# Stick-breaking scores copied to SBUF by ScalarE, the running sum subtracted from the copy; softplus and its sum share a place

## The chip, the core and the metric

The kernel runs on one core of a Trainium2 chip. The metric is the device time of one execution in microseconds, the median of several runs. The core's engines run at the same time, each through its own list of instructions in order: TensorE (PE, with its weight loads as PEld), VectorE (DVE), ScalarE (ACT), GpSimd (POOL), and SyncE (SP), which issues most DMAs. An instruction waits on semaphores for what it needs from another engine. Matmuls write to PSUM, where this kernel keeps eight tiles of 128 x 512 floats (called banks below); the rest of the working data is in SBUF.

## The reference

One decoder layer on a sequence of 512 positions with width 2048. Two attention groups of 16 heads each work on one projection of the normed input, a sliding-window group A and a stick-breaking group B. Their normed outputs go through one output projection, and a squared-ReLU MLP follows. The change is in group B, which for a block of 128 queries is:

```python
z = einsum('bqhd,bshd->bhqs', q_blk, k) * scale
log_beta = log_sigmoid(z)
log_1m = where(causal, log_sigmoid(-z), 0.0)
later = cumsum(log_1m, axis=3, reverse=True) - log_1m
w = where(causal, exp(log_beta + later), 0.0)
out = einsum('bhqs,bshd->bqhd', w, v)
```

With softplus(z) = -log_sigmoid(-z) and log_sigmoid(z) = z - softplus(z), the exponent of w is z minus the sum of softplus from the end of the row to this position, this one included. That is the form that the kernel computes: softplus as max(z, 0) + ln(1 + exp(-|z|)), its running sum from the right, and exp(z - sum).

## The kernel before, in words

Everything is in float32; the large products are made of three matmuls each, from high and low parts of both operands (`mm3`, lines 113 to 118; the parts come from a cast on ACT, L91, and a subtraction on DVE, L92, whose tiles are called `hi_...` and `lo_...`). The stages follow each other: input norm, group A's projections and attention, group B's, output projection, MLP. PE runs the large projections all the time, and the attention is threaded through them: after every second 128-row tile of a projection `pump()` starts or ends one unit of attention.

A unit of group B is one block of queries i (0 to 3) of one pair of heads c (0 to 7), the two heads being the two halves s = 0 and 1. `begin(i)` computes the scores of both halves into two PSUM banks (`scores`, L549, six matmuls in all) and calls `weights`. `end(i)`, one or more pumps later, transposes the weights on PE through two more banks (`wtr`, L583), copies them on DVE to the pair's tiles `wt` (L584), and after block 3 multiplies by v (`bv`, L600). A block is (i + 1) * 128 wide. Pairs 0 to 3 run from about 325 to 456 us, beside projections `ps_v` and `ps_qk`; pairs 4 to 7 from about 500 to 632 us. The handover from one pair to the next inside such a group has block 3 of the one and block 0 of the next in flight at once.

The weights of one half take ten steps: on ACT Abs of z, Exp and Ln (L562 to L564, into tile `a`); on DVE the softplus from z and a (L565, into tile `b`); on GpSimd a select that zeroes the part of the diagonal block that is not causal (L566); on DVE the scan from the right (L569, back into `a`) and the subtraction z - a (L571, into `b`); on GpSimd a select that fills the non-causal part with -1e30 (L572); on ACT the last Exp (L574). The scores z stay in their PSUM bank until L571 has read them. The banks of all these short-lived tiles come from one pool of four (`bank`, tag `pa`), so the next tile that gets a bank waits for the last reader of the tile before it. The SBUF tiles `a` and `b` have two buffers for each tag: `wa` and `wb` for half 0, `wc` and `wd` for half 1.

The order on each engine is not written out: the framework's scheduler makes it from the program and its dependencies, and so can put steps of the two halves and of other work between each other. It is fixed when the program is built.

Of the kernel before, what the change touches and what calls it, by code (L numbers as in the profile page):

```python
# [12 lines left out]
F32 = mybir.dt.float32  # L13
F32R = mybir.dt.float32r
AF = mybir.ActivationFunctionType
ALU = mybir.AluOpType
# [4 lines left out]
P = 128  # L21
# [37 lines left out]
def hymba_layer(ctx: ExitStack, tc: tile.TileContext, x, norm_attn_g, w_in, q_norm_g, k_norm_g,  # L59
                sinks, rel_bias, swa_out_g, sb_out_g, w_out, norm_mlp_g, w_up, w_down, sel, eye, out):  # L60
    nc = tc.nc
    x, out = x[0], out[0]
# [21 lines left out]
    wk = attn.enter_context(tc.tile_pool(name="wk", bufs=2, side="right"))  # L84
# [455 lines left out]
    def sb_pair(c, q, k, vs, keep):  # L540
# [12 lines left out]
        def weights(i, sc):  # L553
            w = (i + 1) * P
            dg = slice(i * P, (i + 1) * P)
            ws = []
            for s in range(2):
                z = sc[s][:, 0:w]
                a = wk.tile([P, 512], F32, tag=("wa", "wc")[s], name=f"a{c}_{i}{s}")[:, 0:w]
                b = wk.tile([P, 512], F32, tag=("wb", "wd")[s], name=f"b{c}_{i}{s}")[:, 0:w]  # L560

                nc.scalar.activation(out=a, in_=z, func=AF.Abs)  # L562
                nc.scalar.activation(out=a, in_=a, func=AF.Exp, scale=-1.0)
                nc.scalar.activation(out=a, in_=a, func=AF.Ln, bias=1.0)  # L564
                nc.vector.scalar_tensor_tensor(out=b, in0=z, scalar=0.0, in1=a, op0=ALU.max, op1=ALU.add)  # L565
                nc.gpsimd.affine_select(out=b[:, dg], in_=b[:, dg], pattern=[[-1, P]], compare_op=ALU.is_gt,  # L566
                                        fill=0.0, base=0, channel_multiplier=1)

                nc.vector.tensor_tensor_scan(out=a[:, ::-1], data0=ones2[:, 0:1].broadcast_to([P, w]),  # L569
                                             data1=b[:, ::-1], initial=0.0, op0=ALU.mult, op1=ALU.add)  # L570
                nc.vector.tensor_tensor(out=b, in0=z, in1=a, op=ALU.subtract)  # L571
                nc.gpsimd.affine_select(out=b[:, dg], in_=b[:, dg], pattern=[[-1, P]], compare_op=ALU.is_gt,  # L572
                                        fill=NEG, base=0, channel_multiplier=1)
                nc.scalar.activation(out=b, in_=b, func=AF.Exp)  # L574
                ws.append(b)
            return ws

        def turn(i, ws):
# [8 lines left out]
        def begin(i):  # L587
            ws_of[i] = weights(i, scores(i))
# [27 lines left out]
    for o in range(2):  # L616
        vs = v_group(o)
        for hq in range(2):
# [12 lines left out]
            for pr, (q, k) in enumerate(((q0, k0), (q1, k1))):  # L631
                c = 2 * qd + pr
# [284 lines left out]
    wd = w_down.rearrange("(g r p) n -> r p g n", r=2, p=P)  # L917
# [125 lines left out]
    for cj in range(2 * NC):  # L1043
        c, j = divmod(cj, 2)
# [7 lines left out]
        for s, (name, ai, _, b, more) in enumerate(d_products(cj)):  # L1052
# [27 lines left out]
            if not more:  # L1080
                pool, tag = ((pa, "pa"), (pp, "pp"))[b // 2]
                banks[b] = [pool.tile([P, 512], F32, tag=tag, name=f"ps_d{q}{tt}") for tt in range(2)]
            a = act[c, ai]
# [45 lines left out]
```

## Time and profile before

| | |
|---|---|
| median of 3 runs | 2007.57 us (2007.29 to 2007.81) |
| profiled execution | 2007.77 us, its span 2006.0 us |
| PE busy | 1978.6 us, 99% |
| DVE busy | 1643.7 us, 82% |
| ACT busy | 1037.7 us, 52% |
| GpSimd busy | 1020.5 us, 51% |
| TensorE's granted clock, mean | 0.998 |

Busy time of the four engines adds up to much more than the span, since they overlap. An engine's share is a mean over stages, so what a step costs is read from the stretch in which it runs. In a timeline row the first number is the start in microseconds from the start of the span, the second the length from the first start to the last end of a group of equal instructions in a row ("x2" is two of them), and the brackets name the idle time ahead of it and what ended that.

### The profile page before, as it was taken

Reading aid. Unit: us, or ns where it says so; the run is one execution under the profiler, and the core shown is the slowest. Engines: PE = TensorE matmul, PEld = TensorE weight load, DVE = VectorE, ACT = ScalarE, POOL = GpSimd, SP = SyncE. Lnnn points to the kernel's source line nnn. Section 1 sums busy time; section 2 is a strip of 40 time slices with the busy share of each in tenths; the row PEclk is TensorE's granted clock in tenths of the full one; section 3 lists DMA queues with packets and bytes.
Section 4 is the critical chain, followed back from the end, with each engine's and each line's share of the span. In section 5 each row is a group of like instructions: output and inputs, shape, how many; then the busy total and the mean of one; then the engine's idle time right before and its main releaser. Section 6 shows DMA issues by size and latency. Waiting matters only on the chain.

```text
span 2006.0 us, 31353 instructions
## 1 busy us (share of the span) xinstructions
PE 1978.6 (99%) x11652; PEld 1718.5 (86%) x11652; DVE 1643.7 (82%) x2136; ACT 1037.7 (52%) x1900; POOL 1020.5 (51%) x904
## 2 busy tenths in 40 slices
PE   8999999999999999999999999999999999999998
PEld 7877777778777889999999999998888888888887
DVE  4459754664776479999999999998999999999987
ACT  6357544553654575656565656565443333334443
POOL 0013341221321038777777777775866656656664
PEclk9999999999999999999999999999999999999999
DMA  6742332224245555665656565656766457457451
GB/s 223 114 138 85 95 103 80 81 69 136 87 140 171 196 168 179 216 203 188 204 187 208 183 212 180 215 179 251 274 250 248 159 230 283 158 223 270 147 189 63
DMA packets 213916, 350.31 MB, mean 175 GB/s; under 512 B 9779, under 2 KB 154372, under 8 KB 206596
## 3 DMA queue, kind: packets, MB, share of 16 engines
q1 hardware_dynamic: 211216, 345.02, 50.7%
q10 hardware_dynamic: 2548, 3.30, 1.4%
q8 instruction: 91, 1.49, 0.3%
q14 instruction: 61, 0.50, 0.1%
HBM read 270.16 MB, written 78.12 MB: 174 GB/s over the span
## 4 chain that ended last, share of the span: by engine, by line
PE 85%; DVE 6%; ACT 3%; DMA 3%; POOL 2%; issue 1%; SPq 0%; POOLq 0%; ACTq 0%; DVEq 0%
PE ps_u L823 10%; PE ps_u L822 10%; PE ps_u L821 10%; PE ps_d L1094 9%; PE ps_d L1095 9%; PE ps_d L1093 9%; PE ps_qk L116 3%; PE ps_qk L118 3%; PE ps_qk L117 3%; PE ps_o L118 2%; PE ps_o L116 2%; PE ps_o L117 2%; DMA skew<-rv 2%; PE bv L600 1%; DVE a L569 1%
## 5 line engine op out<-in xcount | busy, mean ns | idle before, releaser
L823 PE MATMUL ps_u<-h2h,lo_u 128*128 128x256 f32 x1792 | 507.2, 283 | 0.6 <-DVE lo_u L92 0.6
L821 PE MATMUL ps_u<-h2h,hi_u 128*128 128x256 f32 x1792 | 507.4, 283 | 0.0
L822 PE MATMUL ps_u<-h2l,hi_u 128*128 128x256 f32 x1792 | 507.1, 283 | 0.0
L1093 PE MATMUL ps_d<-hi_d,ad 128*128 128x512 f32 x896 | 349.4, 390 | 4.1 <-DMA ad<-ac 2.9
L1094 PE MATMUL ps_d<-lo_d,ad 128*128 128x512 f32 x896 | 349.5, 390 | 1.6 <-DVE lo_d L92 1.6
L1095 PE MATMUL ps_d<-hi_d,ad 128*128 128x512 f32 x896 | 349.2, 390 | 0.0
L823 PEld LDWEIGHTS ps_u<-h2h,lo_u 128*128 128x128 f32 x1792 | 344.0, 192 | 0.8 <-DVE lo_u L92 0.8
L822 PEld LDWEIGHTS ps_u<-h2l,hi_u 128*128 128x128 f32 x1792 | 344.0, 192 | 0.0
L821 PEld LDWEIGHTS ps_u<-h2h,hi_u 128*128 128x128 f32 x1792 | 344.0, 192 | 0.0
L797 POOL TENSOR_TENSOR s_u<-st_u 128x256 f32<-128x256 f32 x256 | 212.1, 849 | 243.5 <-DVE lo_u L92 175.4
L92 DVE TENSOR_TENSOR lo_d<-T,hi_d 128x1024 fp32r<-128x1024 f32 x128 | 245.7, 1934 | 27.6 <-ACT hi_d L91 27.0
L955 POOL TENSOR_TENSOR T<-st_d,T 128x1024 f32<-128x1024 f32 x64 | 173.8, 2719 | 183.9 <-DVE lo_d L92 179.0
L92 DVE TENSOR_TENSOR lo_u<-s_u,hi_u 128x512 fp32r<-128x512 f32 x256 | 262.5, 1026 | 0.3 <-ACT hi_u L91 0.3
L91 ACT CAST hi_u<-st_u 128x384 fp32r<-128x384 f32 x256 | 131.2, 513 | 228.8 <-PE ps_u L822 223.3
L91 ACT CAST hi_d<-T 128x1024 fp32r<-128x1024 f32 x128 | 134.8, 1055 | 194.5 <-PE ps_d L1095 182.1
L92 DVE TENSOR_TENSOR lo_u<-st_u,hi_u 128x384 fp32r<-128x384 f32 x256 | 194.5, 760 | 30.8 <-ACT hi_u L91 29.9
L1093 PEld LDWEIGHTS ps_d<-hi_d,ad 128*128 128x128 f32 x896 | 168.6, 188 | 40.0 <-ACT e L847 3.3
L92 DVE TENSOR_TENSOR lo_d<-st_d,hi_d 128x1024 fp32r<-128x1024 f32 x96 | 194.7, 2040 | 8.7 <-ACT hi_d L91 8.5
L1094 PEld LDWEIGHTS ps_d<-lo_d,ad 128*128 128x128 f32 x896 | 168.5, 188 | 37.2 <-DVE lo_d L92 2.3
L1095 PEld LDWEIGHTS ps_d<-hi_d,ad 128*128 128x128 f32 x896 | 168.6, 188 | 35.1
L91 ACT CAST hi_d<-st_d 128x1024 fp32r<-128x1024 f32 x96 | 101.2, 1055 | 150.8 <-PE ps_d L1095 135.1
L91 ACT CAST hi_u<-s_u 128x512 fp32r<-128x512 f32 x256 | 158.5, 619 | 18.2 <-POOL s_u L797 18.2
(243 smaller groups left out, 3824.1 us busy)
## 6 DMA issues: line engine op xcount, KB each, us to landing
st_u<-in_w_up SPq DMA_DIRECT2D x128, 512.0 KB, 3.7
st_d<-in_w_down SPq DMA_DIRECT2D x64, 1024.0 KB, 8.3
ad<-ac SPq DMA_DIRECT2D x56, 1024.0 KB, 6.5
ac<-ah SPq DMA_DIRECT2D x32, 896.0 KB, 3.8
ac<-al SPq DMA_DIRECT2D x32, 896.0 KB, 5.8
st_qk<-in_w_in SPq DMA_DIRECT2D x64, 256.0 KB, 3.0
st_o<-in_w_out SPq DMA_DIRECT2D x32, 512.0 KB, 4.2
st_qa<-in_w_in SPq DMA_DIRECT2D x16, 512.0 KB, 3.8
```

Of the source, the lines that this page charges most:

```text
L91: nc.scalar.copy(out=hi, in_=st)
L92: nc.vector.tensor_tensor(out=lo, in0=st, in1=hi.bitcast(F32), op=ALU.subtract)
L116: nc.tensor.matmul(ps, ah, bh, start=first, stop=False)
L117: nc.tensor.matmul(ps, ah, bl, start=False, stop=False)
L797: last_sum[0] = nc.gpsimd.tensor_tensor(out=o, in0=a, in1=b, op=op)
L821: nc.tensor.matmul(o, wh[:, a], hh[:, b], start=first, stop=False, skip_group_check=True)
L822: nc.tensor.matmul(o, wh[:, a], hl[:, b], start=False, stop=False, skip_group_check=True)
L823: nc.tensor.matmul(o, wl[:, a], hh[:, b], start=False, stop=(k == KP - 1), skip_group_check=True)
L955: nc.gpsimd.tensor_tensor(out=o, in0=raw[cj, a, h], in1=raw[cj, b, h], op=ALU.subtract)
L1093: nc.tensor.matmul(o, al, bh[:, kk], start=first, stop=False, skip_group_check=True)
L1094: nc.tensor.matmul(o, al, bl[:, kk], start=False, stop=False, skip_group_check=True)
L1095: nc.tensor.matmul(o, ar, bh[:, kk], start=False, stop=end, skip_group_check=True)
```

## The change

Three things change in `weights`. ACT copies the scores z from PSUM to a tile `lw` in SBUF, one more instruction for each half (64 in all), written between Exp and Ln. The subtraction and what follows it work on `lw` in place, so z is no longer read after the softplus and the copy. The softplus tile `b` now comes from the same tag as `a` (`wa` or `wc`), and `lw` takes the tag that `b` had: with two buffers for a tag, the `a` of the next block of that half takes the place of this block's `b`. From L564 on the line numbers of the changed kernel are one higher.

```diff
--- before.py
+++ after.py
@@ -556,11 +556,12 @@
             ws = []
             for s in range(2):
                 z = sc[s][:, 0:w]
-                a = wk.tile([P, 512], F32, tag=("wa", "wc")[s], name=f"a{c}_{i}{s}")[:, 0:w]
-                b = wk.tile([P, 512], F32, tag=("wb", "wd")[s], name=f"b{c}_{i}{s}")[:, 0:w]
+                a, b = [wk.tile([P, 512], F32, tag=("wa", "wc")[s], name=f"{n}{c}_{i}{s}")[:, 0:w] for n in "ab"]
+                lw = wk.tile([P, 512], F32, tag=("wb", "wd")[s], name=f"lw{c}_{i}{s}")[:, 0:w]
 
                 nc.scalar.activation(out=a, in_=z, func=AF.Abs)
                 nc.scalar.activation(out=a, in_=a, func=AF.Exp, scale=-1.0)
+                nc.scalar.copy(out=lw, in_=z)
                 nc.scalar.activation(out=a, in_=a, func=AF.Ln, bias=1.0)
                 nc.vector.scalar_tensor_tensor(out=b, in0=z, scalar=0.0, in1=a, op0=ALU.max, op1=ALU.add)
                 nc.gpsimd.affine_select(out=b[:, dg], in_=b[:, dg], pattern=[[-1, P]], compare_op=ALU.is_gt,
@@ -568,11 +569,11 @@
 
                 nc.vector.tensor_tensor_scan(out=a[:, ::-1], data0=ones2[:, 0:1].broadcast_to([P, w]),
                                              data1=b[:, ::-1], initial=0.0, op0=ALU.mult, op1=ALU.add)
-                nc.vector.tensor_tensor(out=b, in0=z, in1=a, op=ALU.subtract)
-                nc.gpsimd.affine_select(out=b[:, dg], in_=b[:, dg], pattern=[[-1, P]], compare_op=ALU.is_gt,
+                nc.vector.tensor_tensor(out=lw, in0=lw, in1=a, op=ALU.subtract)
+                nc.gpsimd.affine_select(out=lw[:, dg], in_=lw[:, dg], pattern=[[-1, P]], compare_op=ALU.is_gt,
                                         fill=NEG, base=0, channel_multiplier=1)
-                nc.scalar.activation(out=b, in_=b, func=AF.Exp)
-                ws.append(b)
+                nc.scalar.activation(out=lw, in_=lw, func=AF.Exp)
+                ws.append(lw)
             return ws
 
         def turn(i, ws):
```

The scheduler orders the engines' lists anew. In the rows below names end in block and half (`z_30` is block 3, half 0), then a buffer number. First DVE at the handover from pair 1 to pair 2, block 3 and then the copies of `wt` of block 2, before:

```order
L565 SCALAR_TENSOR_TENSOR b_30_3675<-z_30_3666,a_30_3674 128x512
L565 SCALAR_TENSOR_TENSOR b_31_3688<-z_31_3667,a_31_3687 128x512
L569 SCALAR_TENSOR_TENSOR a_30_3674<-ones_494,b_30_3675 128x512
L569 SCALAR_TENSOR_TENSOR a_31_3687<-ones_494,b_31_3688 128x512
L571 TENSOR_TENSOR b_30_3675<-z_30_3666,a_30_3674 128x512
L571 TENSOR_TENSOR b_31_3688<-z_31_3667,a_31_3687 128x512
L584 COPY wt_0_3568<-wtr_20_3712 128x3x128
L584 COPY wt_1_3569<-wtr_21_3717 128x3x128
L92 TENSOR_TENSOR lo_qk_0_3973<-st_qk_0_3969,hi_qk_0_3972 128x1024
```

The same place on DVE in the changed program:

```order
L566 SCALAR_TENSOR_TENSOR b_30_3703<-z_30_3694,a_30_3702 128x512
L585 COPY wt_0_3592<-wtr_20_3744 128x3x128
L570 SCALAR_TENSOR_TENSOR a_30_3702<-ones_494,b_30_3703 128x512
L566 SCALAR_TENSOR_TENSOR b_31_3718<-z_31_3695,a_31_3717 128x512
L572 TENSOR_TENSOR lw_30_3704<-lw_30_3704,a_30_3702 128x512
L570 SCALAR_TENSOR_TENSOR a_31_3717<-ones_494,b_31_3718 128x512
L585 COPY wt_1_3593<-wtr_21_3749 128x3x128
L572 TENSOR_TENSOR lw_31_3719<-lw_31_3719,a_31_3717 128x512
L92 TENSOR_TENSOR lo_qk_0_4017<-st_qk_0_4013,hi_qk_0_4016 128x1024
```

The steps of the two halves alternate now, and the copies of `wt` for block 2 stand among them, ahead of the second subtraction instead of behind it; `lo_qk_0` follows the second subtraction.

ACT at the same handover, from the last Exp of block 3 to the Ln of the next pair's block 0, before:

```order
L574 ACTIVATE b_30_3675<-b_30_3675 128x512
L562 ACTIVATE a_00_3748<-z_00_3740 128x128
L574 ACTIVATE b_31_3688<-b_31_3688 128x512
L563 ACTIVATE a_00_3748<-a_00_3748 128x128
L562 ACTIVATE a_01_3761<-z_01_3741 128x128
L564 ACTIVATE a_00_3748<-a_00_3748 128x128
L563 ACTIVATE a_01_3761<-a_01_3761 128x128
L564 ACTIVATE a_01_3761<-a_01_3761 128x128
```

The same place on ACT in the changed program:

```order
L575 ACTIVATE lw_30_3704<-lw_30_3704 128x512
L562 ACTIVATE a_00_3780<-z_00_3772 128x128
L564 COPY lw_00_3782<-z_00_3772 128x128
L563 ACTIVATE a_00_3780<-a_00_3780 128x128
L562 ACTIVATE a_01_3795<-z_01_3773 128x128
L565 ACTIVATE a_00_3780<-a_00_3780 128x128
L575 ACTIVATE lw_31_3719<-lw_31_3719 128x512
L563 ACTIVATE a_01_3795<-a_01_3795 128x128
L564 COPY lw_01_3797<-z_01_3773 128x128
L565 ACTIVATE a_01_3795<-a_01_3795 128x128
```

The last Exp of half 1 (`lw_31`) has moved behind the first Ln of block 0, and an Exp, a copy and a Ln of block 0's half 1 stand behind it.

PE at the first scores of the next pair, before:

```order
L118 MATMUL ps_v_3338<-hi_v_5_3724,hT_364 128x512
L549 MATMUL z_00_3740<-hl_b_3315,hl_b_3259 128x256 x3
L549 MATMUL z_01_3741<-hl_b_3315,hl_b_3259 128x256 x3
L116 MATMUL ps_v_3339<-hi_v_5_3724,hT_356 128x512
L117 MATMUL ps_v_3339<-lo_v_5_3725,hT_356 128x512
```

The same place on PE in the changed program:

```order
L118 MATMUL ps_v_3350<-hi_v_5_3756,hT_364 128x512
L549 MATMUL z_00_3772<-hl_b_3327,hl_b_3267 128x256
L549 MATMUL z_01_3773<-hl_b_3327,hl_b_3267 128x256
L549 MATMUL z_00_3772<-hl_b_3327,hl_b_3267 128x256
L549 MATMUL z_01_3773<-hl_b_3327,hl_b_3267 128x256
L549 MATMUL z_00_3772<-hl_b_3327,hl_b_3267 128x256
L549 MATMUL z_01_3773<-hl_b_3327,hl_b_3267 128x256
L116 MATMUL ps_v_3351<-hi_v_5_3756,hT_356 128x512
```

The six matmuls of the two halves' scores alternate, where the three of one half stood ahead of the three of the other.

## Rows read from the trace of the kernel before

**Rows 1.** The page: span, and busy time of each engine with its share.

```profile
span 2006.0 us, 31353 instructions
...
PE 1978.6 (99%) x11652; PEld 1718.5 (86%) x11652; DVE 1643.7 (82%) x2136; ACT 1037.7 (52%) x1900; POOL 1020.5 (51%) x904
```

**Rows 2.** Window: length, then busy time of PE, PEld, DVE, ACT, POOL.

```profile
325.00:640.00 315.00, 307.95 (x1497) 233.72 (x1496) 208.83 (x342) 166.27 (x347) 78.23 (x147) 1.00 0.34 107
```

**Rows 3.** Waits of PE, 320 to 640 us: in total, times, longest.

```profile
PE z L549 <- DVE b L571: 3.6, 6, 0.7
PE z L549 <- DVE wt L584: 1.5, 2, 0.8
PE wtr L583 <- ACT b L574: 1.2, 2, 1.1
```

**Rows 4.** Timeline of PE: around first scores, undisturbed and at a handover.

```profile
331.20 0.39 PE L118 MATMUL ps_qk<-hT,lo_qk 128*128 128x512 f32 x1
...
332.07 0.50 PE L116 MATMUL ps_qk<-hT,hi_qk 128*128 128x512 f32 x1
...
386.32 0.39 PE L118 MATMUL ps_v<-hi_v,hT 128*128 128x512 f32 x1
387.35 1.21 PE L549 MATMUL z<-hl_b,hl_b 64*128 64x256 f32 x6 [0.65 <-DVE b L571]
388.50 0.50 PE L116 MATMUL ps_v<-hi_v,hT 128*128 128x512 f32 x1
```

**Rows 5.** Timeline of DVE at the handover: start, length, shape, count.

```profile
382.95 1.29 DVE L565 SCALAR_TENSOR_TENSOR b<-z,a 128x512 f32<-128x512 f32 x2 [1.84 <-ACT a L564]
384.15 2.56 DVE L569 TENSOR_TENSOR_SCAN a<-ones,b 128x512 f32<-128x512 f32 x2
386.63 1.26 DVE L571 TENSOR_TENSOR b<-z,a 128x512 f32<-128x512 f32 x2
387.81 1.01 DVE L584 COPY wt<-wtr 128x384 f32<-128x384 f32 x2
388.74 1.22 DVE L92 TENSOR_TENSOR lo_qk<-st_qk,hi_qk 128x1024 fp32r<-128x1024 f32 x1
389.87 0.63 DVE L565 SCALAR_TENSOR_TENSOR b<-z,a 128x128 f32<-128x128 f32 x2
...
391.44 0.47 DVE L571 TENSOR_TENSOR b<-z,a 128x128 f32<-128x128 f32 x2
392.03 1.29 DVE L584 COPY wt<-wtr 128x512 f32<-128x512 f32 x2
```

**Rows 6.** Timeline of ACT at the same handover.

```profile
380.27 1.09 ACT L562 ACTIVATE a<-z 128x512 f32<-128x512 f32 x2
...
388.45 0.62 ACT L574 ACTIVATE b<-b 128x512 f32<-128x512 f32 x1
...
389.86 0.31 ACT L564 ACTIVATE a<-a 128x128 f32<-128x128 f32 x1
```

**Rows 7.** Timeline of GpSimd's selects, and of DVE's lo_v split beside the first.

```profile
354.75 1.22 DVE L92 TENSOR_TENSOR lo_v<-st_v,hi_v 128x1024 fp32r<-128x1024 f32 x1
...
354.90 1.21 POOL L566 TENSOR_SCALAR_AFFINE_SELECT b<-b 128x128 f32<-128x128 f32 x1 [0.24 <-DVE b L565]
...
384.37 1.09 POOL L566 TENSOR_SCALAR_AFFINE_SELECT b<-b 128x128 f32<-128x128 f32 x1 [0.31 <-DVE b L565]
...
388.03 0.29 POOL L572 TENSOR_SCALAR_AFFINE_SELECT b<-b 128x128 f32<-128x128 f32 x1 [0.30 <-DVE b L571]
```

**Rows 8.** Lines of DVE by form, 560 to 900 us: busy, mean ns.

```profile
L863 DVE TENSOR_TENSOR al<-u,ah 128x512 fp32r<-128x512 f32 x7 | 4.7, 676 | 0.0
...
L571 DVE TENSOR_TENSOR b<-z,a 128x512 f32<-128x512 f32 x6 | 3.8, 673 | 0.0
```

**Rows 9.** Timeline of PE: end of that pair.

```profile
391.39 1.03 PE L583 MATMUL wtr<-ident,b 128*128 128x128 f32 x8
...
392.83 0.64 PE L600 MATMUL bv<-wt,v 128*64 128x512 f32 x1
```

## The prediction

> **What bounds the kernel now.** I read the page first: TensorE (PE) is busy for 1978.6 of 2006.0 us, 99%, every other engine for 82% or less [rows 1]. So a change off PE is worth what it does to PE's few waits. The windows come next: in the stretch of the stick-breaking units, 325 to 640 us, PE is busy for 307.95 of 315, VectorE (DVE) for 208.83, ScalarE (ACT) for 166.27 [rows 2]. Not more than about 7 us of idle time lies there. The view of waits names it [rows 3]: the first scores z of a unit wait for the subtraction of an earlier unit (six times, 3.6 us), for a copy of wt (twice, 1.5 us), and the transposes wtr wait for the last exponential (twice, 1.2 us).
>
> The timeline of PE shows what one such wait costs beyond its idle time [rows 4]. Undisturbed, from the matmul ahead of the scores (331.20) to the one behind them (332.07) it takes 0.87 us. At 387 us, where pair 1's block 3 hands over to pair 2's block 0, it takes 388.50 - 386.32 = 2.18 us: 0.65 us of idle time and 0.6 us because the scores run three and three rather than interleaved. That is 1.3 us at each of four handovers (387, 419, 561, 593 us). The two others of the six waits, with the two on wt, lie at the pairs that begin a group of four (345 and 519 us): 1.2 + 1.5 = 2.7 us idle in both, with the same 0.5 us of serial scores 1.9 us each. If every wait of this list vanished, the gain would be 4 x 1.3 + 2 x 1.9 = 9.0 us, with half a microsecond more at the last pair's scores (about 618 us): **9.5 us is the most that can be won**.
>
> **What is removed.** The bank of z is read last by the copy and the softplus, not by the subtraction, which stands behind the scan. At the handover the softplus group starts at 382.95 and the subtraction ends at 386.63 + 1.26 = 387.89 [rows 5]. PE wants the banks at about 386.55, so released by 384.9 they make PE wait for nothing. I count all 9.5 us as gone. The matmuls and DMAs stay the same in number, and no queue of SP is moved past anything that waits.
>
> **What is added on ACT.** 64 copies, one for each half of each unit. The trace has none, but Abs reads the same tile and writes as much: a pair of 512 wide takes 1.09 us, 0.55 each [rows 6]. So it is at most 64 x 0.55 = 35 us, on an engine with 149 us free in this stretch. It costs only where it stands in a chain. In block 3, abs, copy and exp of half 0 and abs of half 1 now stand ahead of the first Ln, before only four Abs and Exp: one longer step in either case, nearly the same start.
>
> **What is moved on DVE.** The order of the changed program shows three things. The softpluses, scans and subtractions of the two halves alternate, and both copies of wt of block 2, which stood behind the second subtraction, now stand ahead of it. By the starts of the groups in rows 5 the four steps last 1.20 + 2.48 + 1.18 + 0.93 = 5.8 us. Before, the subtractions end after the first three; now the last one ends after all four: 0.93 us later. Block 2 has the same change at a smaller size (one copy of wt, about 0.4, and a select that is held, about 0.4, below), so ACT begins block 3 about 0.8 us later, at 381.05 where it was 380.27 [rows 6], and the softplus starts some 0.75 later. With 0.1 for a select that waits for the first subtraction, the last subtraction ends at 387.89 + 0.75 + 0.93 + 0.1 = about 389.65.
>
> **What becomes slower in itself.** A select on GpSimd takes 0.29 us when it is alone (388.03) [rows 7]. The one that starts at 354.90 beside the split lo_v on DVE (354.75 to 355.97, two operands in SBUF) takes 1.21, and ends 0.14 after it; the one at 384.37, beside a scan (two in SBUF), 1.09. Beside the subtraction of before, which reads PSUM, it is 0.29. The subtraction of after reads two tiles of SBUF, and what DVE starts right behind the second one is the split lo_qk, two more. So the select of half 1, which at 388.03 ran beside a copy from PSUM, will run beside lo_qk: it starts at 389.7, lo_qk at 389.55, and it ends at 390.85. The exponential of half 1, at 388.45 before, starts at 390.95: **2.5 us later**.
>
> [...]
>
> **Who waits for that.** On ACT, behind this exponential, stand in the new order an Exp, a copy and a Ln of the next pair's block 0. The Ln ended at 389.86 + 0.31 = 390.17 [rows 6]; it will end at 390.95 + 0.54 + 0.2 + 0.2 + 0.3 = 392.2. DVE, which takes its instructions in order, stands at that block's second softplus: from there to the end of the second subtraction it is 1.7 us (390.2 to 391.91) [rows 5], and behind it the copies of wt for block 3 (1.29 for the two) that the matmuls bv need. The second ends at 393.32 before, and at 392.2 + 1.7 + 2 x 0.6 = 395.1 after. PE had its transposes at 391.39 and bv at 392.83 [rows 9]. It waits at 390.1 for the transposes of half 1 and then for this copy: the second bv matmul starts 1.8 us later than before, the 1.3 us that PE won at the scores included. **Each handover: +1.8 us rather than -1.3**, four times +7.2. Nothing later gives this back, as PE is the bound.
>
> For the unknown costs both ends, by handover: -1.3 if the select and the copy of wt delay nothing, +2.5 if the whole lateness of the exponential were added. I take +1.8, the sum by the rows.
>
> **The other places.** Last pairs of a group (454 and 628 us): no next pair stands behind, and the transposes of half 1 wait for the held exponential. The subtraction ends 1.76 later, the select is held behind it, and together the exponential comes about 1.4 later than PE wants it; at the second of them the 0.6 us at 618 is won. Together +2.2. First pairs: 1.9 us won at the scores, but about 1.1 us lost at block 2's transposes and 2.8 at block 3's, where 1.06 and 0.17 stand now [rows 3]: about +1.0 each, bounds -2 and +2. Sum: 7.2 + 2.2 + 2.0 = **+11.4 us**. Against the profiled execution (2006.0 span and 1.8 around it, 2007.8) that makes 2019.2; the median is 0.2 below, so **2019.0**.
>
> [...]
>
> **Rivals.** (1) The gain comes as meant. PE's waits on z vanish and no new one comes, because the exponentials end in time. For it: DVE is idle for about a third of the stretch [rows 2]. Against: at the handover DVE has almost no gap from 382.95 to 393.3 [rows 5]. It gives 2007.8 - 9.5 = about 1998. It decides where the copies of wt still start when the transposes are done, as at 392.03. (2) The select comes first, or is not held: the exponential of half 1 is then about 0.8 earlier at each place. Handovers cost +1.0, the last pairs some +1, the first pairs nothing: about +5, 2012.5. (3) The lateness of block 2 does not add, and the alternating order is hidden: each handover +0.2, all else about nothing: +1, 2008.5. Its condition is that the copies of wt of block 2 start where DVE would have been idle anyway. (4) The first pairs are at their upper bound and the handovers too, with 0.4 us more at 561 and 593, where more of DVE's work stands between: 4 x 2.5 + 2 x 2 + 2.2 = +16, 2024.
>
> **How the numbers follow.** My forecast has a chance of 0.50, rival 2 0.20, rival 3 0.13, rival 1 0.12, rival 4 0.05. A measurement of this kernel can tell about 0.2% (4 us) from no change. Slower holds the forecast, rival 4 and most of rival 2: 0.70. Same holds rival 3 and what is left of rival 2: 0.18. Faster holds rival 1: 0.12. The range, 2006 to 2024, leaves out rival 1 and the tail above; the likeliest case's own is 2014 to 2022.
>
> **What would show it.** Right: between 325 and 640 us the waits of z on DVE are gone, and in their place the profile names waits of bv on the copies of wt and of wtr on the exponential, two to three microseconds at each handover; the second select of block 3 takes about 1.2 us beside lo_qk rather than 0.29; the stretch is 11 us longer and the rest unchanged. Wrong: the selects behind the subtraction stay at 0.29 us, or PE's idle time in the stretch falls under 7 us.

## The result, and the profile after

Slower, and by more than forecast. The changed kernel takes 2035.37 us (median of 4 runs, 2033.47 to 2037.40) against 2007.43 us of the kernel before; the ratio is 1.0138, with a 95% interval of 1.0126 to 1.0151. That is +27.9 us where the forecast was +11.4, outside the range of 2006 to 2024. The profiled execution is the fastest of the four, 2033.47 us.

The page of the changed kernel answers to [rows 1]:

```profile
span 2031.8 us, 31453 instructions
...
PE 1985.4 (98%) x11652; PEld 1718.9 (85%) x11652; DVE 1645.1 (81%) x2136; ACT 1059.6 (52%) x1964; POOL 1021.2 (50%) x904
```

The span grew by 2031.8 - 2006.0 = 25.8 us. PE is idle for 2031.8 - 1985.4 = 46.4 us where it was 27.4, 19.0 more, and busy for 6.8 us more with the same 11652 matmuls. These two parts are kept apart below.

Windows over the same 1434 matmuls, from the second scores of pair 0 to the end of bv of pair 7, first in the kernel before and then in the changed one, show where this lies (length, then busy time of PE, PEld, DVE, ACT, POOL, then TensorE's granted clock, share of the DMA engines and GB/s):

```profile
331.52:632.51 300.99, 293.94 (x1434) 222.66 (x1433) 203.49 (x331) 160.01 (x333) 75.87 (x142) 1.00 0.34 107
```

```profile
327.29:655.47 328.18, 300.41 (x1434) 222.74 (x1433) 204.79 (x331) 181.59 (x395) 77.80 (x142) 0.97 0.32 99
```

This stretch is 27.2 us longer. The rest, where the change has nothing, is 1.5 us shorter in these two executions: 4.2 us less ahead of the stretch and 2.7 more behind it.

The waits of PE from 320 to 660 us (total, times, longest) answer to [rows 3]:

```profile
PE wtr L584 <- ACT lw L575: 19.6, 11, 2.8
PE bv L601 <- DVE wt L585: 6.7, 4, 1.7
```

All eight waits of scores on DVE are gone, as the forecast had it. In their place PE waits eleven times for a last Exp, mostly that of half 1, and four times for a copy of wt ahead of bv: 26.3 us where 6.3 stood. The handover that the forecast worked out is on PE's timeline (start, length, what; the brackets name the idle time ahead and what ended it), against [rows 4, 9]:

```profile
385.08 0.62 PE L549 MATMUL z<-hl_b,hl_b 64*128 64x256 f32 x6
...
388.53 0.60 PE L584 MATMUL wtr<-ident,lw 128*128 128x128 f32 x4
390.74 0.66 PE L584 MATMUL wtr<-ident,lw 128*128 128x128 f32 x4 [1.61 <-ACT lw L575]
...
393.54 2.96 PE L601 MATMUL bv<-wt,v 128*64 128x512 f32 x16 [1.68 <-DVE wt L585]
```

The scores run interleaved and without a wait, in 0.62 us, and PE then waits 1.61 us for the transposes of half 1 and 1.68 us for bv. On DVE, against [rows 5]:

```profile
382.64 0.69 DVE L566 SCALAR_TENSOR_TENSOR b<-z,a 128x512 f32<-128x512 f32 x1 [2.01 <-ACT a L565]
383.25 0.55 DVE L585 COPY wt<-wtr 128x384 f32<-128x384 f32 x1
383.79 1.23 DVE L570 TENSOR_TENSOR_SCAN a<-ones,b 128x512 f32<-128x512 f32 x1
384.93 0.67 DVE L566 SCALAR_TENSOR_TENSOR b<-z,a 128x512 f32<-128x512 f32 x1
385.51 0.68 DVE L572 TENSOR_TENSOR lw<-lw,a 128x512 f32<-128x512 f32 x1
386.37 1.31 DVE L570 TENSOR_TENSOR_SCAN a<-ones,b 128x512 f32<-128x512 f32 x1 [0.18 <-POOL b L567]
387.61 0.53 DVE L585 COPY wt<-wtr 128x384 f32<-128x384 f32 x1
388.06 0.68 DVE L572 TENSOR_TENSOR lw<-lw,a 128x512 f32<-128x512 f32 x1
388.66 1.21 DVE L92 TENSOR_TENSOR lo_qk<-st_qk,hi_qk 128x1024 fp32r<-128x1024 f32 x1
...
392.80 1.28 DVE L585 COPY wt<-wtr 128x512 f32<-128x512 f32 x2
```

The last subtraction ends at 388.74, and 388.74 - 382.64 = 6.10 us lie between the first softplus and that, where rows 5 give 387.89 - 382.95 = 4.94. On ACT, against [rows 6]:

```profile
380.02 0.58 ACT L562 ACTIVATE a<-z 128x512 f32<-128x512 f32 x1
...
390.05 0.63 ACT L575 ACTIVATE lw<-lw 128x512 f32<-128x512 f32 x1 [1.80 <-POOL lw L573]
...
390.93 0.31 ACT L565 ACTIVATE a<-a 128x128 f32<-128x128 f32 x1
```

On GpSimd, against [rows 7]:

```profile
385.72 0.62 POOL L567 TENSOR_SCALAR_AFFINE_SELECT b<-b 128x128 f32<-128x128 f32 x1 [1.97 <-DVE b L566]
...
388.87 1.16 POOL L573 TENSOR_SCALAR_AFFINE_SELECT lw<-lw 128x128 f32<-128x128 f32 x1 [2.25 <-DVE lw L572]
```

The select of half 1 takes 1.16 us beside lo_qk, and the last Exp starts at 390.05, as the forecast described it. The other select here, of the softplus of half 1, takes 0.62 us beside the first subtraction, and the scan at 386.37 waits 0.18 us for it; the sum had 0.1 for this.

Timelines of two kernels don't stand at the same time, so a chain is best read from where it starts. The table takes for each kernel the four handovers inside a group (pairs 1, 2, 5 and 6) and gives means in us: from the first scores of block 3 on PE to its first Abs; from its first softplus to the end of its last subtraction; from there to the last Exp; and from the scores to the end of the last copy of wt. All are differences of starts and ends of timeline rows; for the kernel before, pair 1, they are 380.27 - 379.27, 387.89 - 382.95, 388.45 - 387.89 (0.56) and 393.32 - 379.27 [rows 5, 6], where 379.27 is the start of block 3's scores:

```profile
379.27 1.05 PE L549 MATMUL z<-hl_b,hl_b 64*128 64x512 f32 x6
```

The last column, "clock", is an estimate of what the lower clock took: one minus the mean granted clock of an execution, times its span, as a mean over the executions. It counts time at half clock as half lost, and is good to about 1 us.

| kernel | time, us | scores to Abs | softplus to subtraction | to last Exp | scores to last copy | clock |
|---|---|---|---|---|---|---|
| before | 2007 | 1.02 | 4.95 | 0.55 | 14.0 | 4 |
| changed | 2035.4 | 2.43 | 6.10 | 1.32 | 16.5 | 16 |
| subtraction from PSUM, new order | 2017.3 | 2.07 | 5.73 | 1.32 | 15.8 | 4 |
| subtraction from PSUM, old order | 2018.2 | 1.29 | 5.87 | 0.55 | 15.4 | 9 |
| subtraction from SBUF, old order | 2021.6 | 1.91 | 5.88 | 0.88 | 16.1 | 9 |
| new order, masked first | 2018.0 | 1.70 | 6.07 | 0.03 | 14.9 | 7 |
| old order, copies behind both Ln | 2012.7 | 1.13 | 4.95 | 0.72 | 14.2 | 7 |

Abs to softplus is 2.6 to 2.7 us in all of them, so the first half's Ln is not later. The whole chain is 2.5 us longer, 1.4 of it before block 3 has begun: its Abs stands in ACT's list behind the last Exp of block 2, and that is late for the same reasons.

What the places cost PE is read from the second scores of one pair to those of the next (for a last pair, to the end of its bv), again from starts and ends of timeline rows:

| place | before, us | changed, us | more, in all | forecast |
|---|---|---|---|---|
| first pairs (0 and 4) | 34.41, 34.28 | 37.15, 37.53 | 6.0 | 2.0 |
| handovers (1, 2, 5, 6) | 32.23, 32.25, 32.82, 32.24 | 34.51, 36.48, 35.73, 36.03 | 13.2 | 7.2 |
| last pairs (3 and 7) | 27.74, 28.32 | 31.60, 32.39 | 7.9 | 2.2 |

The other part, PE's longer busy time, is a lower clock. At the last pair of the first group, where no next pair stands behind, PE waits for the transposes of half 1, and bv follows:

```profile
458.71 0.60 PE L584 MATMUL wtr<-ident,lw 128*128 128x128 f32 x4
461.79 0.65 PE L584 MATMUL wtr<-ident,lw 128*128 128x128 f32 x4 [2.48 <-ACT lw L575]
...
462.86 4.17 PE L601 MATMUL bv<-wt,v 128*64 128x512 f32 x16
```

These 16 products take 4.17 us, the same 16 at 393.54 take 2.96. The windows there (the third figure from the right is the granted clock, as a part of full speed):

```profile
450.00:460.00 10.00, 9.31 (x46) 7.51 (x45) 7.81 (x12) 6.11 (x11) 1.56 (x5) 1.00 0.18 54
460.00:470.00 10.00, 8.21 (x35) 5.89 (x36) 3.34 (x4) 2.64 (x4) 2.36 (x2) 0.83 0.39 131
...
464.00:466.00 2.00, 2.00 (x8) 1.25 (x7) 0.30 (x1) 0.00 (x0) 0.00 (x0) 0.50 0.19 58
```

Ahead of the wait the clock is at 1.00, behind it at 0.50, and from 467 us on at 1.00 again. In the kernel before no stretch of 10 us between 320 and 660 us is below 1.00; in the changed kernel eight are, from 0.83 to 0.98, and five of its eight bv groups take 4.2 to 4.9 us. Each of those five has a wait of 1.73 to 2.82 us for the transposes shortly ahead; at 390.74 and 578.86 waits of 1.61 and 1.77 us, each with one of 1.68 behind it, were followed by products at full clock. At the eighth pair the low clock falls on the transposes and the projection instead, and its bv takes 3.12 us:

```profile
650.45 1.11 PE L584 MATMUL wtr<-ident,lw 128*128 128x128 f32 x4 [2.75 <-ACT lw L575]
...
650.50:653.50 3.00, 3.00 (x10) 1.73 (x12) 1.82 (x2) 0.83 (x1) 0.00 (x0) 0.50 0.61 178
```

So six times in this stretch the clock is at 0.50, for about 3.4 us each (462.8 to 466.2 us at the fourth pair). By an estimate (half of 6 x 3.4 us) this takes 10 of the stretch's 27 us, more than the 6.8 us of busy time: the scores, which run interleaved now, keep PE busy for less (0.62 us where a handover had 1.21), and hide a part of it. The four executions were granted 0.991 to 0.993 on the mean, the kernel before 0.998; in the table that is 12 of the 28 us.

### The profile page after: what moved, and what is told of

Same layout as the page of the kernel before. It is cut to its first block, busy times and chain, and to the rows that moved or that the text cites. A ratio compares the mean times of both kernels' runs of the same rounds, so it can differ in the third digit from the quotient of the medians.

```text
span 2031.8 us, 31453 instructions
## 1 busy us (share of the span) xinstructions
PE 1985.4 (98%) x11652; PEld 1718.9 (85%) x11652; DVE 1645.1 (81%) x2136; ACT 1059.6 (52%) x1964; POOL 1021.2 (50%) x904
## 3 DMA queue, kind: packets, MB, share of 16 engines
q8 instruction: 91, 1.49, 0.3%
## 4 chain that ended last, share of the span: by engine, by line
PE 83%; DVE 6%; ACT 4%; DMA 3%; POOL 2%; issue 1%; SPq 0%; POOLq 0%; ACTq 0%; DVEq 0%
PE ps_u L824 10%; PE ps_u L823 10%; PE ps_u L822 10%; PE ps_d L1095 10%; PE ps_d L1094 10%; PE ps_d L1096 10%; PE ps_qk L116 2%; PE ps_qk L118 2%; PE ps_qk L117 2%; PE ps_o L118 2%; PE ps_o L116 2%; PE ps_o L117 2%; DVE a L570 2%; DMA skew<-rv 2%; PE bv L601 2%
## 5 line engine op out<-in xcount | busy, mean ns | idle before, releaser
L91 ACT CAST hi_u<-s_u 128x512 fp32r<-128x512 f32 x256 | 158.5, 619 | 18.3 <-POOL s_u L798 18.2
```

The source lines that it names most:

```text
L91: nc.scalar.copy(out=hi, in_=st)
```

## The experiments

**One part alone.** Of the change only the shared place; no copy, the subtraction reads z:

```diff
-                nc.scalar.copy(out=lw, in_=z)
-                nc.vector.tensor_tensor(out=lw, in0=lw, in1=a, op=ALU.subtract)
+                nc.vector.tensor_tensor(out=lw, in0=z, in1=a, op=ALU.subtract)
```

> One part alone: softplus b and its running sum a share a place (same tag, two buffers), the subtraction writes lw, but it reads z from PSUM and there is no copy on ScalarE. The lists of VectorE and TensorE stand as in the kernel before. Theory A (the new order, the copy's place in ScalarE's list and the held second select make the loss, the sharing of places nothing): 2003 to 2011 us, the waits of the scores on the subtraction as before (3.6 us, six times). Rival C (the shared place stalls ScalarE, since the next block's Abs needs this block's scan to be done): 2015 us or more, with Abs waiting for the scan.

Measured: 2007.95 us, ratio 1.0004 (0.9994 to 1.0014), PE's waits on the subtraction 4.0 us, seven times. The shared place costs nothing, rival C falls.

**One operand put back.** The changed kernel with the copy made and not used:

```diff
-                nc.vector.tensor_tensor(out=lw, in0=lw, in1=a, op=ALU.subtract)
+                nc.vector.tensor_tensor(out=lw, in0=z, in1=a, op=ALU.subtract)
```

> The changed kernel with one operand put back: the copy on ScalarE is made and is not used, the subtraction reads z from PSUM. VectorE's order stays that of the changed kernel. Theory A: the loss stays, 2028 to 2045 us, since the subtraction of half 1 still ends behind both copies of wt and its select still runs beside the split lo (about 1.2 us); the early release of the banks is gone as well, so waits of the scores on the subtraction come back. Rival B (the subtraction with two operands in SBUF, which holds GpSimd's selects, makes the loss): 2005 to 2012 us.

Measured: 2017.26 us, ratio 1.0045 (1.0028 to 1.0062). Neither theory: 18 of the 28 us go with the operand, 10 stay. By the table's estimate 12 of the 18 are the clock, which stayed at 1.00 in the whole stretch of the profiled execution. DVE's order at the handovers is the changed kernel's; at the first pairs of the groups it differs. DVE and GpSimd at the same handover show what went:

```profile
385.05 0.68 DVE L572 TENSOR_TENSOR lw<-z,a 128x512 f32<-128x512 f32 x1
385.64 1.21 DVE L570 TENSOR_TENSOR_SCAN a<-ones,b 128x512 f32<-128x512 f32 x1
...
385.26 0.29 POOL L567 TENSOR_SCALAR_AFFINE_SELECT b<-b 128x128 f32<-128x128 f32 x1 [1.97 <-DVE b L566]
...
388.04 1.15 POOL L573 TENSOR_SCALAR_AFFINE_SELECT lw<-lw 128x128 f32<-128x128 f32 x1 [1.09 <-DVE lw L572]
```

The select beside the subtraction takes 0.29 us where it took 0.62, and the scan follows the subtraction at once. The select beside lo_qk still takes 1.15, so that one belongs to the order and not to the operand.

**The mask first.** The select that fills with -1e30 works on the copy, ahead of the subtraction:

```diff
                 nc.scalar.copy(out=lw, in_=z)
+                nc.gpsimd.affine_select(out=lw[:, dg], in_=lw[:, dg], ..., fill=NEG, ...)
...
                 nc.vector.tensor_tensor(out=lw, in0=lw, in1=a, op=ALU.subtract)
-                nc.gpsimd.affine_select(out=lw[:, dg], in_=lw[:, dg], ..., fill=NEG, ...)
```

> The changed kernel with the second select moved: it fills the copy lw with -1e30 ahead of the subtraction, beside ScalarE's Exp and Ln, so that the last Exp follows the subtraction with no step on GpSimd between. VectorE's order stays. Theory A: the last exponential of half 1 at a handover comes about 1.4 us earlier (a select of 1.16 us and one hop less), the wait of the transposes of 1.6 to 2.8 us falls under 1.2 at each place, and the lower granted clock behind these waits goes: 2008 to 2018 us. Rival (the order alone makes the loss, the held select is hidden behind it): 2027 us or more.

Measured: 2018.01 us, ratio 1.0055 (1.0039 to 1.0070), at the upper end of theory A. The last Exp starts 0.03 us behind the subtraction rather than 1.32; the stretch from softplus to subtraction stays at 6.07. The held second select is a good part of the loss, and not all; by the table some 9 of the 17 us won are the clock.

**The order of before, in part.** Edges that set the issue order alone put the copies of wt behind the second subtraction and the splits behind those; the halves still alternate:

```diff
+        behind(nc.vector.tensor_tensor(out=lo, in0=st, in1=hi.bitcast(F32), op=ALU.subtract), copies, 4)
...
+                subs.append(nc.vector.tensor_tensor(out=lw, in0=lw, in1=a, op=ALU.subtract))
...
+                cp = behind(nc.vector.tensor_copy(out=wt[s][:, 0:i + 1, i * P:w],
+                                                  in_=tr[:, 0:w].rearrange("p (j q) -> p j q", q=P)), subs, 1)
```

> The changed kernel with VectorE's order of before at the two places that moved: by edges that set the issue order alone, the copies of wt stand behind the second subtraction, and the splits lo_v and lo_qk behind the copies, as in the kernel before. Steps of the two halves still alternate; copy, subtraction from SBUF and early release of the banks stay. Theory A: the second subtraction ends about 0.9 us earlier, its select runs beside a copy from PSUM at 0.29 us, the waits of the transposes and of bv nearly go, and with the scores' waits gone as well: 1999 to 2009 us. Rival B (the two operands in SBUF, whatever the order): 2025 us or more.

Measured: 2028.33 us, ratio 1.0102 (1.0085 to 1.0118). Theory A missed by 19 us, and the rival's figure was met. The select behind the second subtraction ran in 0.29 us and the last Exp 0.45 us behind it, as meant; still 5.8 us lay between softplus and subtraction, with no copy of wt among them: the two scans wait there 0.46 and 0.19 us for selects, the first in the place where the changed kernel has a copy of wt. So to take the copies out doesn't make that stretch short.

**The order of before, in full.** The same edges, and the steps of both halves grouped as before (here with the subtraction from SBUF):

```diff
+            for z, a, b, lw in hs:
+                mark = behind(nc.vector.tensor_tensor_scan(out=a[:, ::-1], ...), mark)
+            for z, a, b, lw in hs:
+                mark = behind(nc.vector.tensor_tensor(out=lw, in0=lw, in1=a, op=ALU.subtract), mark)
```

> All of the change's data flow (copy, subtraction from SBUF, shared place, early release), with VectorE's order at the handovers the same as before, row for row: softplus of both halves, scan of both, subtraction of both, then the copies of wt, then the split. Theory A (order): block 3's chain at a handover, from the softplus to the last exponential, is back at 4.95 + 0.55 us where the changed kernel has 6.1 + 1.3; 2000 to 2012 us. Rival B (two operands in SBUF, whatever the order): the selects of both halves and the scans still hold each other, 2020 us or more.

> As the run with VectorE's order of before, and the -1e30 select made on the copy ahead of the subtraction, off the chain. By theory A the chain is shorter than before's by the select and one hop (0.45 us), and PE waits for neither the banks nor the last exponential: 1999 to 2008 us, the best of these. Rival (the chain is as long as before's all the same, since ScalarE's list has the copies in it): 2008 to 2014 us.

> As the run with VectorE's order of before, with the subtraction reading z from PSUM; the copy is made and not used, the banks are held until the subtraction. Against the run that reads the copy this gives the cost of the two operands in SBUF under one order: theory A, within 4 us of it; rival B, 8 us or more below it.

Measured: 2021.59 us (1.0060 to 1.0090) with the subtraction from SBUF, 2017.82 (1.0042 to 1.0076) with the mask first as well, 2018.15 (1.0046 to 1.0076) with the subtraction from PSUM. The first meets rival B's figure, but the third should then have been 8 us or more below it and was 3.4. The theory that the order makes the loss falls with the third as well: there DVE's order at the handovers and the operands are those of before, and 11 us are lost with the copies on ACT added (and, at the first pairs, with the forced order). DVE at its handover shows where:

```profile
383.74 0.69 DVE L577 SCALAR_TENSOR_TENSOR b<-z,a 128x512 f32<-128x512 f32 x1 [1.71 <-ACT a L576]
385.27 0.69 DVE L577 SCALAR_TENSOR_TENSOR b<-z,a 128x512 f32<-128x512 f32 x1 [0.83 <-ACT a L576]
385.88 2.56 DVE L581 TENSOR_TENSOR_SCAN a<-ones,b 128x512 f32<-128x512 f32 x2
388.35 1.26 DVE L584 TENSOR_TENSOR lw<-z,a 128x512 f32<-128x512 f32 x2
```

The second softplus waits 0.83 us for its Ln. In rows 5 the two softpluses stand as one group of 1.29 us. ACT does eight operations for the two halves where it did six, and in its list both copies, just under 0.6 us each, stand ahead of half 1's Ln; DVE's stretch is 5.7 to 5.9 us long in either order. The new order reads as the scheduler's way to fill that gap with copies of wt: with the operand in PSUM it costs nothing (2017.3 and 2018.2).

Between the two operands 3.4 us lie in the old order, and 18 in the new one; without the clock, by the table, 3 and 6.

**The copies behind both Ln.** The grouped kernel, and on ACT an edge that puts both copies behind the second Ln:

```diff
-                nc.scalar.copy(out=lw, in_=z)
...
+            for z, a, b, lw in hs:
+                behind(nc.scalar.copy(out=lw, in_=z), ln)
```

> All of the change's data flow and VectorE's order of before, and the two copies put behind the Ln of both halves in ScalarE's list (issue order alone), so that nothing new stands ahead of half 1's Ln. New theory D (the copies delay half 1's Ln by two of their lengths, so its softplus starts some 0.9 us later in block 3, and this grows from block to block; the order and the operand only add to it): the stretch from the softplus of half 0 to the end of half 1's subtraction in block 3 goes from 5.88 back to about 5.0 us, and the time to 2004 to 2010 us, against 2021.6 with the copies ahead. Rival B (two operands in SBUF): stays over 2017 us.

> The same with the -1e30 select on the copy ahead of the subtraction, so that no step of GpSimd stands between subtraction and last Exp. Theory D: block 3's chain is 0.4 to 0.5 us shorter than before's, and the banks are free early: PE's waits in the stretch fall from 6.3 to some 3 us, 2001 to 2006 us, faster than the kernel before. Rival (the bank's release was never worth anything, and the selects made on the copy beside the scans hold VectorE): 2007 us or more.

> The run with the copies behind both Ln, with VectorE's order of before forced only outside the first pair of each group of four (there the scheduler's own order stays), since in that run the pair from 498 us on took 4 us longer than before. Theory D: the handovers stay equal to before's (the wait on the banks has become one on wt of the same length), and the first pairs come within 1 us of before's: 2005 to 2010 us, no gain although the banks are free early. Rival (the early release is worth what the waits were, 9.5 us): under 2002 us.

Measured: 2012.72 us (ratio 1.0029, 1.0018 to 1.0041), 2011.93 (1.0023, 1.0014 to 1.0032) and 2013.71 (1.0028, 1.0018 to 1.0039). DVE at the handover of the first of them:

```profile
379.44 1.29 DVE L576 SCALAR_TENSOR_TENSOR b<-z,a 128x512 f32<-128x512 f32 x2 [1.89 <-ACT a L575]
380.64 2.56 DVE L582 TENSOR_TENSOR_SCAN a<-ones,b 128x512 f32<-128x512 f32 x2
383.12 1.27 DVE L585 TENSOR_TENSOR lw<-lw,a 128x512 f32<-128x512 f32 x2
```

The two softpluses are one group of 1.29 us again, and the stretch is 383.12 + 1.27 - 379.44 = 4.95 us: theory D is shown for the stretch, and 9 us of the 2021.6 went with the copies' place. The three times are 3 to 6 us above the upper ends expected; the second, forecast as faster than the kernel before, met its rival's figure instead. And on PE:

```profile
386.42 1.03 PE L598 MATMUL wtr<-ident,lw 128*128 128x128 f32 x8
...
389.38 2.87 PE L616 MATMUL bv<-wt,v 128*64 128x512 f32 x16 [1.46 <-DVE wt L599]
```

Copy, subtraction from SBUF and early release are all there, no score waits at this handover, and bv waits 1.46 us instead. From the second scores of pair 1 to those of pair 2 it is 32.35 us, and 32.23 in the kernel before. **At a handover the early release is worth nothing**: the wait that was ahead of the scores stands at the other end of the same chain. Masking first brought 0.1 to 0.2 us at the first two handovers and cost 0.3 to 0.4 at the other two; its selects took 0.54 us on the mean, where 0.29 is the median in the kernel before. In the third the profiled execution took 2008.6 us at a mean clock of 0.999, its other seven 2012.3 to 2014.6 at 0.996 to 0.997; so some of what is left of this loss lies in the clock. The rest, in that execution's stretch, lies at the first pairs (1.4 us), the last pairs (1.2) and the handovers (1.0). None of these versions beats the kernel before.

**A longer chain in the kernel before.** Two, and then six, copies in place ahead of the last Exp of half 1 in block 3, with nothing of the change:

```diff
+                if i == 3 and s == 1:
+                    for _ in range(2):
+                        nc.scalar.copy(out=b, in_=b)
                 nc.scalar.activation(out=b, in_=b, func=AF.Exp)
```

> The kernel before with two more copies in place (b to b, 512 wide) on ScalarE ahead of the last exponential of half 1 of block 3: some 1.26 us more on that chain for each of the eight pairs, VectorE's and TensorE's order unchanged but for a few rows. If the chain from block 3's scores to the products is what PE waits for, and PE has no slack at a handover, the time rises by 0.9 to 1.3 us for each pair, 7 to 10 us, and by more where the granted clock falls behind the waits: 2014 to 2021 us. If the chain has slack: under 2010 us.

> The kernel before with six copies in place on ScalarE ahead of the last exponential of half 1 of block 3 (3.2 to 3.8 us more on that chain), against two before. It asks for the clock alone, with none of the change in it. The two copies (1.26 us) added 2.9 us in all, so some 0.9 us of slack lie at a handover: with six, single waits of the transposes of 2 to 3 us at each of eight pairs, 16 to 24 us more idle time. If the waits bring the lower granted clock of the changed kernel, PE's busy time rises by 4 to 10 us above 1978.6 with the same work, and the products bv behind such a wait take over 4 us instead of 2.9: 2024 to 2042 us. If that clock came from something else in the change: busy time within 2 us, 2022 to 2032 us.

Measured: 2010.22 us (ratio 1.0018, 1.0008 to 1.0027) and 2015.33 (1.0035, 1.0021 to 1.0049). With two copies, PE's waits:

```profile
PE z L549 <- DVE b L571: 3.6, 6, 0.7
PE wtr L586 <- ACT b L577: 2.9, 4, 1.1
```

About 10 us were added to eight chains and 2.9 came out, at the edge of the case with slack: at a handover of the kernel before, the last Exp has nearly 1 us of slack (1.26 us were added, and the end of bv is 0.3 us later). With six, the waits stayed short:

```profile
PE z L549 <- DVE b L571: 5.6, 8, 1.5
PE wtr L586 <- ACT b L577: 3.7, 4, 1.1
```

The scheduler had moved the transposes of half 1 behind eight more matmuls at this handover, so both figures expected of this run missed, and it did not tell about the clock.

**The clock by itself.** The same with the next projection matmul kept behind the transposes by an edge, six copies and two:

```diff
         m = nc.tensor.matmul(ps, ah, bh, start=first, stop=False)
+        if turned_last:
+            tc.add_manual_dep(m.ins, turned_last[-1].ins.name,
...
```

> The kernel before with six copies in place on ScalarE ahead of the last exponential of half 1 of block 3, and an edge of issue order that keeps the next projection matmul behind the transposes of half 1, so that PE meets the wait (bv stands two matmuls earlier than in the kernel before). Theory (the waits bring the lower clock): the transposes wait 2 to 3.5 us at each of eight pairs, bv behind them takes over 4 us at most pairs instead of 2.9, windows of 10 us there show a granted clock of 0.83 to 0.93, PE's busy time rises by 4 us or more over 1978.6; 2025 to 2045 us. Rival (something else in the change): the waits come, the clock stays at 1.00 and bv at 2.9; 2022 to 2032 us.

> The same order with two copies instead of six, so that the waits of the transposes are about 2.1 us shorter (under 1 us at a handover). Theory: clock at 1.00 in all windows of the stretch, bv at 2.9 us, busy time within 2 us of 1978.6; 2009 to 2019 us.

Measured: 2046.53 us (ratio 1.0181, 1.0157 to 1.0204), PE busy for 1994.5 us, and 2016.12 (1.0040, 1.0025 to 1.0055), busy for 1983.9. PE with six copies, behind a long wait and behind a short one, and the windows there:

```profile
363.87 1.11 PE L592 MATMUL wtr<-ident,b 128*128 128x128 f32 x4 [5.96 <-ACT b L583]
364.92 5.25 PE L611 MATMUL bv<-wt,v 128*64 128x512 f32 x16
...
400.59 0.66 PE L592 MATMUL wtr<-ident,b 128*128 128x128 f32 x4 [1.49 <-ACT b L583]
```

```profile
360.00:370.00 10.00, 6.13 (x20) 3.31 (x20) 2.02 (x3) 3.72 (x8) 0.00 (x0) 0.66 0.17 52
364.00:365.00 1.00, 1.00 (x5) 0.67 (x6) 0.00 (x0) 0.00 (x0) 0.00 (x0) 0.50 0.26 88
400.00:410.00 10.00, 9.41 (x46) 6.07 (x47) 2.85 (x6) 4.58 (x12) 1.87 (x3) 1.00 0.26 82
```

Behind 5.96 us the clock is at 0.50 and bv takes 5.25 us; behind 1.49 us it is at 1.00. The windows below 1.00 in this stretch all lie at or right behind the four waits of 3.88 to 5.96 us (the first and last pairs), none behind the four of 1.45 to 1.49 (the handovers). So the low clock came here with PE's own waits of 3.88 us and more, in a kernel with nothing of the change, though the waits were not the 2 to 3.5 us at all eight pairs that were expected. With two copies it was expected to stay at 1.00: one wait of 3.21 us was followed by 0.83 for 10 us, and another window of 0.83 (520 to 530 us) came with no single wait over 0.8 us near it.

The length of one wait doesn't decide it in these runs. In the changed kernel a wait of 1.73 us, with one of 1.68 behind it, was followed by 0.50. With the mask first, waits of up to 2.55 us left the clock at 1.00 in the whole stretch of the profiled execution (0.999 on the mean of its span); with the order of before in part, PE waited 2.50 us at each of the four handovers, and at two of them the clock went to 0.50 (0.992 on the mean). What decides is not shown by these runs.

## Why the prediction was right or wrong

- **The direction and the mechanism of the waits: right.** The waits of the scores went, waits for the last Exp and the copies of wt came, the select beside lo_qk took 1.16 us where about 1.2 was forecast, and the block's end came later than what PE won. The size was wrong: the stretch grew by 27.2 us where the sum had 11.4, and every one of its three places was put too low.
- **The clock: no term of the sum, and the step that failed by most.** By the estimates above it took 10 of the 27 us in the stretch, and 12 of the 28 by the means of all executions; without it the stretch grew by 17. The forecast had new waits of two to three microseconds at each handover and did not ask what the clock does behind them. In the rows of this stretch nothing showed it: the clock was at 1.00 there, and the longest wait 1.06 us. But the trace of the kernel before shows it elsewhere, in group A's projections, behind a wait of the length that was forecast (a second one, of 2.94 us, is at 1392.86):

```profile
110.16 0.59 PE L116 MATMUL ps_qa<-hT,hi_qa 128*128 128x512 f32 x1 [2.79 <-DVE f_q L321]
...
110.50:113.50 3.00, 3.00 (x8) 2.32 (x7) 2.25 (x5) 2.76 (x6) 0.00 (x0) 0.50 0.81 298
```

- **Block 2's lateness, 0.8 us: too small.** Block 3's Abs starts 1.2 to 1.9 us later behind its scores, 1.4 on the mean, and at the handovers the last copy of wt ends 2.5 us later, where the sum had 1.8. Every block is longer and each next one begins behind the last Exp of the one before. The sum of the handovers lacked 6 us: two low stretches of the clock take some 3.4 of them by the estimate, and this lateness (0.6 us too small, four times) most of the rest.
- **"It costs only where it stands in a chain ... one longer step in either case, nearly the same start": wrong for half 1.** It holds for half 0. For half 1 two copies stand ahead of the Ln. In the order of before its softplus is then 0.9 us late in block 3; with the copies moved behind both Ln, 9 us of 2021.6 went. With the copies made and not used, 10 (new order) to 11 us (old order) were lost. In the changed kernel itself DVE doesn't wait for this Ln at the handover: a copy of wt and the scan of half 0 fill the time.
- **"0.93 us later" for the copies of wt moved ahead: about the right size, and not the only cause.** In the changed kernel's rows the stretch grew by 1.15 us, these copies and the 0.18 us behind the select. But without them in it the stretch is 5.77 us, and with the order and the operands of before 5.87. Several causes of nearly the same length lie over each other here, and the sum had one of them.
- **The selects.** The hold by lo_qk was sized rightly at the handovers. The select of the softplus, 0.62 us beside the first subtraction, held the scan for 0.18 us where the sum had 0.1; in block 2 the two scans waited 0.40 and 0.19 us for theirs. With the operand in PSUM the same select took 0.29 us beside that subtraction.
- **"I count all 9.5 us as gone": the waits went, the gain was not there at a handover.** With the chain at its old length, PE loses at bv what it gains at the scores. The bound of a gain has to be taken from the whole chain, not from the wait at one end of it.
- **The last pairs (+2.2 for both) and the first pairs (+2.0).** They took 7.9 and 6.0 us more, with a low clock at each of the four. From block 3's scores to the end of bv the last pairs took 18.2 and 19.0 us where it was 14.4 and 14.7.
- **Rivals.** The gain, the selects that are not held, and the hidden lateness didn't happen. No handover shows a select of half 1 that comes first: there, and at the last pairs, it started 0.2 us behind the split and took 1.16 us. The fourth had the right places: its 16 us are near the 17 that the stretch lost without the clock.

What stays open: which of PE's waits are followed by the low clock. And, of the operand in SBUF, what makes the 6 us that it costs in the new order without the clock, where it costs 3 in the old one. In rows it is the select beside the first subtraction, which the old order doesn't have there, and at the first pairs another order altogether. It was not taken apart further.

## What to carry to other kernels

When two halves share an engine's list, an operation added per half delays the second half by both (its softplus waited 0.83 us here): write out that half's list up to the step that is waited for. A wait that a buffer's release ends is worth removing only where the chain that it belongs to has slack at its other end; before counting it, follow that chain to the next point where the bounding engine meets it. And where a change makes the bounding engine wait longer at a time, its clock can be a term of its own: here, by the estimate, 10 of 27 us.

## What the runs showed of the hardware

- TensorE's granted clock was at 0.50 behind six of the eight pairs' waits of 1.61 to 2.82 us in the changed kernel, and back at 1.00 some 3.4 us later; the 16 products of five pairs took 4.17 to 4.93 us there, and 5.25 behind a wait of 5.96 us in the kernel before with six copies, rather than 2.96. It was not so in each execution: in the profiled execution with the mask first, none of the waits of up to 2.55 us was followed by it (0.999 on the mean of its span).
- A subtraction of 128x512 from SBUF takes 676 ns (mean of 16 in the changed kernel), as the 673 from PSUM in [rows 8]. The select of the softplus beside it took 0.62 us, 0.29 in the run with the operand put back, and the scan behind waited 0.18 us for it. The 16 of 128x384 took 637 ns on the mean, 541 from PSUM in the kernel before; the one at 339.84, beside a GpSimd instruction of 1.38 us (L317), took 1.28 us.
